# Layer 1's neighbourhood attention ends in spare places, the second gated tile is split later, and its buffers are dealt out anew

## The chip, the cores and the metric

The kernel runs on one core of a Trainium2 chip. The time is the device time of one execution in microseconds (us). TensorE is called PE, VectorE DVE, ScalarE ACT, GpSimd POOL, and SyncE, which issues most of the loads, SP. PEld is TensorE's loading of weights, which overlaps with its matmuls.

## The reference

Two layers of a transformer trunk with two token mixers side by side. The latent stream x has 512 tokens, the context 256, the model width is 1024. Each layer normalises and modulates, makes ten groups of columns with one projection, runs neighbourhood attention (NA) and grouped-query attention (GQA), multiplies each by a gate of its own, projects both, adds them under sigmoid gates and projects once more:

```python
    hx = _rmsnorm(x, norm_g) * (1.0 + scale_x) + shift_x
    px = hx @ w_in
    a_k, a_v, b_k, b_v, a_q, b_q, a_z, b_z, g_a, g_b = _split(px, SPLIT_SIZES)
    ...
    a_att = _na_latent(qa, ka, va, cka, cva, rpb, rows)     # 8 heads of 64, window 8 x 16, and all context keys
    b_att = _gqa_latent(qb, k_all, v_all)                   # 8 query heads, 2 key heads, 768 keys
    ...
    o_a = (a_att * jax.nn.silu(a_z)) @ w_o_a
    o_b = (b_att * jax.nn.silu(b_z)) @ w_o_b
    merged = jax.nn.sigmoid(g_a) * o_a + jax.nn.sigmoid(g_b) * o_b
    x_new = x + gate_x * (merged @ w_out)
```

Layer 0 also computes the context's tokens (update_ctx), with 256 rows more in every stage; layer 1 leaves them out after the keys and values. All is float32.

## The kernel before

**Split products.** PE multiplies operands of the rounded type fp32r. Each float32 operand is therefore split in a high part (an ACT cast to fp32r) and a low part (the rest, a subtraction on DVE or POOL), and each product is made of three matmuls, high by high, high by low and low by high (lines 352 to 354). Weights go through three places: a raw buffer that SP's load fills (`raw`, three buffers), `whi` and `wlo` (rings of eight each, in the pool `wp`). A raw buffer is free when the low part has read it. `load_w` (line 322 the cast, 325 the low part) loads tiles of 512 columns, `load_w2` (337 and 339) two tiles of 256 in one. `mix_lo` gives the low parts of weights to POOL and DVE by turns.

**Layers and stages.** Each layer goes through the projections for NA, NA itself, the projection BKV and BQ for GQA (lines 937 on; w_q is the weight of BQ), GQA, the projections w_o_a and w_o_b with the merge, and w_out. PE is kept busy during attention by pieces of other projections (`fill`): gate chunks, and in GQA the pieces of w_o_a. The flag `first` is true in layer 0.

**Attention.** `pipeline` runs the scores of head h, then the values of head h−1. Scores go to psum tiles `pss`, are reduced to a maximum, and exponentiated by ACT (line 815 for NA, 975 for GQA), four blocks of 128 queries to a head. `softmax_tail` normalises a block: DVE inverts the sum, then DVE (line 667) or POOL (669 and 670; the blocks 1 and 3 of each head) multiplies. `transpose_split` transposes four blocks on PE into a psum tile `pst` of two buffers, ACT casts it to `pth` (687) and DVE makes `ptl` (688); the value matmuls (837 to 848 for NA, 990 and 991 for GQA) add up in one psum tile `psv`. An NA head has four such tiles, two of 512 columns, then two of 448; a GQA head has six. `head_out` evacuates psv: an ACT copy of one half (696), a DVE add (698) and a product with the gate's values on POOL (699) into `za` or `zb`. The tile `ho` has one buffer, so the next copy waits for the product; psv has one buffer, so the next head's first value matmul waits for the add (in layer 0 the context's queries use it as well, lines 762 and 763).

In layer 1, the last head of GQA uses a *spare place* for every other one of its tiles (line 676): psum of the scores (`pss`), and `whi`/`wlo` from the weights' ring. So more than two transposed tiles can be under way. `att["end"]` switches it on.

**Gated tiles.** `hilo` splits the gated values za and zb in high (`gah`, `gbh`) and low (`gal`, `gbl`) parts, four pieces of 128 channels each, on ACT and POOL. These, `tg` (the gates), `gk`, `qb` and others have the same size (128 x 3072 float32) and share nine buffers (`big`): a new tile waits for the last reader of the one whose buffer it gets. `early` runs before the last head's values of GQA and splits the first three pieces of zb; the last piece follows after the pool of attention is closed.

**Order.** The instructions are emitted in program order and then placed by the framework's scheduler on each engine, which runs its own in sequence and waits for others by semaphores. `ordered(x, name)` ties an instruction behind another of the same engine, and makes it wait for nothing else. The numbers of buffers in a ring are dealt out in program order, so a tile that is allocated earlier in the program pushes all later tiles of its ring back.

## Time and profile before

| | us |
|---|---|
| median of 3 runs | 1142.38 (1141.61 to 1142.96) |
| profiled execution | 1141.48 |
| its span, first to last instruction | 1139.6 |
| PE busy | 1119.0 (98%) |
| DVE busy | 816.4 (72%) |
| ACT busy | 581.1 (51%) |
| POOL busy | 492.7 (43%) |
| moved by DMA | 135.09 MB, mean 119 GB/s |

Layer 0's attention ends near 560 us of the span, its merge lies behind that, layer 1's NA runs to about 883 us and its GQA to about 1070 us. A row of the timeline has the start, the duration, the engine, the source line, the operation, the tiles written and read, their size, and in brackets how long the engine was idle before it and what ended that. "x3" stands for three in a row. The durations of matmuls reach past the next one's start, as they are pipelined: the pace of PE is read from start to start.

### The profile page before, as it was taken

What the parts mean: (1) busy time and instruction counts of PE and PEld (TensorE: products, weight loads), DVE (VectorE), ACT (ScalarE), POOL (GpSimd) and SP (SyncE); (2) the same over time, 40 slices, a digit from 0 to 9 for tenths busy, and PEclk for the clock granted to TensorE, in tenths of its full rate; (3) what the DMA queues carried; (4) which work ended last, traced back from release to release, by engine and by line L of the source; (5) the groups of instructions that cost most, each with busy time, mean ns of one, the idle gap of its engine ahead of it and who ended that gap; (6) DMA issues with size and microseconds to landing.
All of it is one profiled execution on the core that took longest, in us unless ns stands there. A gap on an engine that the chain in (4) does not pass through costs nothing.

```text
span 1139.6 us, 17434 instructions
## 1 busy us (share of the span) xinstructions
PE 1119.0 (98%) x6128; PEld 947.5 (83%) x6128; DVE 816.4 (72%) x1537; ACT 581.1 (51%) x1185; POOL 492.7 (43%) x467
## 2 busy tenths in 40 slices
PE   7999999999999999999999999999999999999998
PEld 5788888888988888888888887888887988888777
DVE  6777688887554786698588755569787666798783
ACT  6553366665433565666330365337666445665531
POOL 2073354544374343353512427246553664363521
PEclk9999999999999999999999999999999999999999
DMA  9645222333333232461343524634332333141343
GB/s 370 238 127 157 81 61 70 97 115 98 114 102 89 91 108 87 80 242 38 137 141 102 176 75 116 188 91 125 103 111 74 112 94 110 66 157 38 99 163 99
DMA packets 90863, 135.09 MB, mean 119 GB/s; under 512 B 10804, under 2 KB 55064, under 8 KB 90136
## 3 DMA queue, kind: packets, MB, share of 16 engines
q1 hardware_dynamic: 88640, 127.57, 35.2%
q0 software_dynamic: 1856, 6.29, 1.7%
q8 instruction: 48, 0.79, 0.3%
q14 instruction: 39, 0.32, 0.1%
q10 hardware_dynamic: 280, 0.12, 0.0%
HBM read 116.63 MB, written 17.32 MB: 118 GB/s over the span
## 4 chain that ended last, share of the span: by engine, by line
PE 86%; DVE 5%; DMA 3%; issue 3%; POOL 2%; ACT 1%; SPq 0%; POOLq 0%; ACTq 0%; DVEq 0%
PE psx L352 12%; PE psx L354 12%; PE psx L353 12%; PE psf L352 10%; PE psf L354 10%; PE psf L353 10%; PE pst L683 5%; PE pss L807 3%; PE pss L734 2%; PE pss L735 2%; PE psv L990 2%; PE psv L991 2%; PE pst L432 1%; DMA rawb<-in_w_ada_dram 1%; DVE ptl L688 1%
## 5 line engine op out<-in xcount | busy, mean ns | idle before, releaser
L687 ACT CAST pth<-pst 128x512 fp32r<-128x512 f32 (+1 forms) x173 | 97.2, 576 | 96.4 <-PE pst L683 56.0
L688 DVE TENSOR_TENSOR ptl<-pst,pth 128x512 fp32r<-128x512 f32 (+1 forms) x173 | 113.8, 671 | 41.1 <-ACT pth L687 40.0
L339 POOL TENSOR_TENSOR wlo<-raw,whi 128x512 fp32r<-128x512 f32 x68 | 95.9, 1414 | 104.4 <-ACT whi L337 86.2
L352 PE MATMUL psf<-hx,whi 128*128 128x512 f32 (+1 forms) x368 | 140.1, 381 | 0.0
L353 PE MATMUL psf<-hx,whi 128*128 128x512 f32 (+1 forms) x368 | 138.0, 375 | 0.0
L352 PE MATMUL psx<-whi,hx 128*128 128x512 f32 (+1 forms) x368 | 137.8, 375 | 0.0
L354 PE MATMUL psf<-hx,wlo 128*128 128x512 f32 (+1 forms) x368 | 137.7, 374 | 0.0
L354 PE MATMUL psx<-whi,hx 128*128 128x512 f32 (+1 forms) x368 | 135.9, 369 | 0.0
L353 PE MATMUL psx<-wlo,hx 128*128 128x512 f32 (+1 forms) x368 | 135.3, 368 | 0.0
L337 ACT CAST whi<-raw 128x512 fp32r<-128x512 f32 x136 | 82.5, 621 | 55.9 <-DMA raw<-in_w_in_dram 36.5
L322 ACT CAST whi<-raw 128x512 fp32r<-128x512 f32 x88 | 54.0, 622 | 100.9 <-PE psx L354 35.3
L683 PE MATMUL pst<-ident,p 128*128 128x128 f32 x628 | 97.7, 272 | 0.8 <-DVE r L664 0.6
L669 POOL TENSOR_SCALAR r<-r 128x1 f32<-128x1 f32 x64 | 22.3, 348 | 164.1 <-DVE r L664 139.4
L339 DVE TENSOR_TENSOR wlo<-raw,whi 128x512 fp32r<-128x512 f32 x68 | 67.1, 989 | 32.9 <-ACT whi L337 32.6
L325 POOL TENSOR_TENSOR wlo<-raw,whi 128x512 fp32r<-128x512 f32 x36 | 50.7, 1413 | 85.6 <-ACT whi L322 72.4
L683 PEld LDWEIGHTS pst<-ident,p 128*128 128x128 f32 x628 | 76.4, 140 | 12.3 <-PE psv L763 0.7
L670 POOL TENSOR_TENSOR p<-p,r 128x512 f32<-128x512 f32 (+1 forms) x64 | 84.3, 1317 | 5.1
L352 PEld LDWEIGHTS psx<-whi,hx 128*128 128x128 f32 x368 | 69.4, 189 | 12.2 <-issue 1.2
L354 PEld LDWEIGHTS psx<-whi,hx 128*128 128x128 f32 x368 | 69.4, 189 | 12.0 <-DVE hx L1165 0.2
L354 PEld LDWEIGHTS psf<-hx,wlo 128*128 128x128 f32 x368 | 69.3, 188 | 11.8
L353 PEld LDWEIGHTS psx<-wlo,hx 128*128 128x128 f32 x368 | 69.5, 189 | 10.7
L352 PEld LDWEIGHTS psf<-hx,whi 128*128 128x128 f32 x368 | 69.4, 189 | 10.4 <-ACT zt L517 0.2
(265 smaller groups left out, 3068.6 us busy)
## 6 DMA issues: line engine op xcount, KB each, us to landing
raw<-in_w_in_dram SPq DMA_DIRECT2D x168, 256.0 KB, 2.9
rawb<-in_w_ada_dram SPq DMA_DIRECT2D x48, 256.0 KB, 2.9
gs<-zt SPq DMA_DIRECT2D x32, 256.0 KB, 2.0
raw<-in_w_out_dram SPq DMA_DIRECT2D x32, 256.0 KB, 3.0
tg<-gs SPq DMA_DIRECT2D x4, 1536.0 KB, 6.5
rawx<-in_w_ada_dram SPq DMA_DIRECT2D x8, 512.0 KB, 7.7
raw<-in_w_o_a_dram SPq DMA_DIRECT2D x16, 256.0 KB, 2.9
raw<-in_w_o_b_dram SPq DMA_DIRECT2D x16, 256.0 KB, 4.3
```

Source lines behind the costliest of these rows:

```text
L322: S.copy(hi[:, :n], raw[:, :n])
L325: e.tensor_tensor(lo[:, :n], raw[:, :n], F(hi[:, :n]), ALU.subtract)
L337: S.copy(hi, raw)
L339: lo_eng(i).tensor_tensor(lo, raw, F(hi), ALU.subtract)
L352: T.matmul(ps, lhs[0], rhs[0], start=first, stop=False)
L353: T.matmul(ps, lhs[0], rhs[1], start=False, stop=False)
L354: T.matmul(ps, lhs[1], rhs[0], start=False, stop=last)
L670: G.tensor_tensor(p[:, c0:c1], p[:, c0:c1], r[:, i:i + 1].to_broadcast([128, c1 - c0]), ALU.mult)
L683: T.transpose(pt[:, c0:c0 + 128], src, ident)
L687: S.copy(hi[:, n0:n1], pt[:, n0:n1])
L688: V.tensor_tensor(lo[:, n0:n1], pt[:, n0:n1], F(hi[:, n0:n1]), ALU.subtract)
L807: T.matmul(pss.rearrange("p (a b n) -> p a b n", a=2, b=2), qi, blocks_of(k, *at), start=b, stop=not b)
```

## The change

1. **Spare places at the end of layer 1's NA.** A new flag `att["last"]` is set when the last head of a pipeline has its values made, also in NA; the count of turns starts anew there. In layer 1 the tiles 1 and 3 of NA's head 7 so take psum of the scores and a `whi`/`wlo` pair. In layer 1, block 3 of head 7 is normalised by DVE, not by POOL.
2. **The split of zb.** In `early` the high parts are tied behind the last exponential of GQA (`att["exp"]`), the low parts behind POOL's last normalisation, in both layers (before: no tie for the high parts, and none for the low ones in layer 0). The last piece is split by column spans, in layer 0 512 and 256, with the low part on DVE in both layers, and the last head's products with zb are on DVE in both layers.
3. **Buffers.** `tg[3]` is allocated and loaded after the second chunk of w_o_b's weights has been asked for, not in `early`. `gbh`, `gbl` and what follows so get other buffers of the nine.
4. **w_o_b's casts.** Those of the chunks 1 to 3 are tied behind the last output copy in layer 0 too.

```diff
@@ -562,7 +562,7 @@
             for f in fs:
                 for a, b in parts or [(0, ntok)]:
                     S.copy(R(dst[0][:, f, a:b]), sv[:, f, a:b])
-                    if hi_after is not None and f > 0:
+                    if hi_after is not None:
                         ordered(ins[-1], hi_after)
                     lo(f).tensor_tensor(R(dst[1][:, f, a:b]), sv[:, f, a:b], dst[0][:, f, a:b], ALU.subtract)
                     if lo_after is not None and lo(f) is G:
@@ -673,7 +673,7 @@
 
             def transpose_split(blocks, n0=0, n1=512):
 
-                spare = att["end"] and not first and att["turn"] % 2 == 1
+                spare = (att["end"] or att["last"]) and not first and att["turn"] % 2 == 1
                 att["turn"] += 1
                 pt = psw(512, "s" if spare else "t")
                 for src, c0 in blocks:
@@ -696,7 +696,7 @@
                 S.copy(t1[m:m + 64, :n], po[o:o + 64, :n])
                 att["ho"] = nc.cur_bb.bb.instructions[-1].name
                 V.tensor_tensor(t1[m:m + 64, :n], po[m:m + 64, :n], t1[m:m + 64, :n], ALU.add)
-                (V if (att["end"] and not first) else G).tensor_tensor(dst, dst, t1[m:m + 64, :n], ALU.mult)
+                (V if att["end"] else G).tensor_tensor(dst, dst, t1[m:m + 64, :n], ALU.mult)
 
             def rows(a, half):
                 return a[64 * half:64 * half + 64]
@@ -814,7 +814,8 @@
                     r = sp.tile([128, 2], F32, tag="r", name=nm("r"), bufs=8)
                     S.activation(p[:, :512], p[:, :512], AF.Exp, bias=mx[:, 0:1], scale=-1.0,
                                  accum_out=r[:, 0:1])
-                    softmax_tail(p, 512, r[:, 0:1], [(0, 512)], G if i in NA_POOL else None)
+                    softmax_tail(p, 512, r[:, 0:1], [(0, 512)],
+                                 G if i in NA_POOL and (first or (h, i) != (7, 3)) else None)
                     ps_.append(p)
                     run(att["bg"], 1)
                 return ps_
@@ -856,6 +857,7 @@
                 prev = None
                 for h in range(8):
                     att["bg"] = bg if h > 3 or pm["n"] == 1 else []
+                    att["last"] = False
                     st = scores_of(h)
                     if prev is not None:
                         values_of(h - 1, prev)
@@ -865,12 +867,12 @@
                     run(fill, len(fill))
                     last()
                 run(bg, len(bg))
-                att["end"] = last is not None
+                att["end"], att["last"], att["turn"] = last is not None, True, 0
                 values_of(7, prev)
                 run(fill, len(fill))
 
             akt = [k_tile(e, True) for e in range(2)]
-            att["end"], att["turn"] = False, 0
+            att["end"], att["last"], att["turn"] = False, False, 0
 
             def na_first(h):
                 j, e = h // 2, h % 2
@@ -973,6 +975,7 @@
                     V.tensor_reduce(mx[:, 0:1], pss, AX, ALU.max, negate=True)
                     r = sp.tile([128, 2], F32, tag="r", name=nm("r"), bufs=8)
                     S.activation(p, pss, AF.Exp, bias=mx[:, 0:1], accum_out=r[:, 0:1])
+                    att["exp"] = next(x.name for x in nc.cur_bb.bb.instructions[::-1] if x.engine == ON_ACT)
                     softmax_tail(p, 768, r[:, 0:1], [(0, 768)], G if i in GQ_POOL else None)
                     ps_.append(p)
                     run(att["bg"], 1)
@@ -1001,11 +1004,10 @@
 
             def early():
 
-                for c in (1, 3):
-                    tg[c] = big("tg")
-                    load_tg(c)
+                tg[1] = big("tg")
+                load_tg(1)
                 gated["b"] = hilo_tiles("gb")
-                hilo(zb, gated["b"], range(3), lo_after=None if first else att["norm"])
+                hilo(zb, gated["b"], range(3), hi_after=att["exp"], lo_after=att["norm"])
             bg = gate_steps((1,), att["p"]) if first else []
             pipeline(fill, 8, gq_first, values_of(zb, gq_values), early, bg)
             gq_es.close()
@@ -1017,7 +1019,7 @@
             for v in range(nv):
                 src = gd[l][8 * v:8 * v + 8].rearrange("k p -> (k p)").unsqueeze(0)
                 nc.sync.dma_start(gv[:, v, :], src.to_broadcast([128, DM]))
-            hilo(zb, gated["b"], [3], None, lambda f: G if first else V)
+            hilo(zb, gated["b"], [3], spans, lambda f: V)
             mg = []
 
             def evac_b(f, n0, n1, ps):
@@ -1034,8 +1036,11 @@
                     at = len(nc.cur_bb.bb.instructions)
                     chunks[i + 1][0]()
                     for x in nc.cur_bb.bb.instructions[at:]:
-                        if not first and x.engine == ON_ACT:
+                        if x.engine == ON_ACT:
                             ordered(x, att["ho"])
+                if i == 0:
+                    tg[3] = big("tg")
+                    load_tg(3)
                 if i % 2 == 0:
                     mg.append(hilo_tiles("m"))
                 for piece in chunks[i][1]:
```

`ordered` is shown above, with `hilo`. The names of psum tiles say their place: `pst` is transposes' own, `pss` the scores'.

The first place is ACT in layer 1 at the end of NA: from head 7's last exponential (line 815) to head 7's output copy before the change. `pth` are the transposed tiles of heads 6 and 7, `ho` the output copies of heads 5, 6 and 7.

```order
L815 ACTIVATE p_2153_9465,r_2155_9468<-p_2153_9465,mx_2154_9466 128x512
L687 CAST pth_2158_9479<-pst_2157_9474 128x512
L696 COPY ho_2124_9366<-psv_2111_9317 64x512
L687 CAST pth_2161_9490<-pst_2160_9485 128x512
L687 CAST pth_2164_9501<-pst_2163_9496 128x448
L687 CAST pth_2167_9514<-pst_2166_9509 128x448
L687 CAST pth_2176_9588<-pst_2175_9583 128x512
L696 COPY ho_2169_9522<-psv_2156_9473 64x512
L687 CAST pth_2179_9599<-pst_2178_9594 128x512
L687 CAST pth_2182_9610<-pst_2181_9605 128x448
L687 CAST pth_2185_9623<-pst_2184_9618 128x448
L696 COPY ho_2187_9631<-psv_2174_9582 64x512
```

And there with the change, from the spare casts of head 7 to head 6's output copy:

```order
L687 CAST whi_2179_9600<-pss_2178_9595 128x512
L687 CAST whi_2185_9624<-pss_2184_9619 128x448
L337 CAST whi_2200_9715<-raw_2199_9713 128x512
L337 CAST whi_2203_9721<-raw_2202_9719 128x512
L337 CAST whi_2206_9727<-raw_2205_9725 128x512
L687 CAST pth_2164_9502<-pst_2163_9497 128x448
L687 CAST pth_2167_9515<-pst_2166_9510 128x448
L337 CAST whi_2209_9733<-raw_2208_9731 128x512
L322 CAST whi_2212_9739<-raw_2211_9737 128x512
L687 CAST pth_2176_9589<-pst_2175_9584 128x512
L322 CAST whi_2215_9745<-raw_2214_9743 128x512
L696 COPY ho_2169_9523<-psv_2156_9474 64x512
```

Head 7's tiles 1 and 3 are cast before head 6's two tiles of 448 columns; eight weight casts (L337 for BKV, L322 for w_q), which stood among the exponentials of heads 5 and 6 and just behind them, now follow the spare casts (six are in these rows).

The second place is ACT at the end of GQA in layer 1, around the last exponential (`p_2685`, L975 before and L977 after); `gbh` is the high part of zb. Before:

```order
L975 ACTIVATE p_2681_11616,r_2683_11619<-pss_2680_11611,mx_2682_11617 128x768
L564 CAST gbh_2713_11753<-zb_2338_10277 128x512 x2
L687 CAST pth_2651_11500<-pst_2650_11495 128x512
L687 CAST pth_2654_11511<-pst_2653_11506 128x512
L687 CAST pth_2657_11522<-pst_2656_11517 128x512
L975 ACTIVATE p_2685_11628,r_2687_11631<-pss_2684_11623,mx_2686_11629 128x768
L687 CAST pth_2660_11533<-pst_2659_11528 128x512
L687 CAST pth_2690_11642<-pst_2689_11637 128x512
L696 COPY ho_2662_11539<-psv_2643_11472 64x512
L687 CAST pth_2693_11653<-pst_2692_11648 128x512
L687 CAST whi_2720_11778<-pss_2719_11773 128x512
L687 CAST whi_2726_11800<-pss_2725_11795 128x512
```

With the change:

```order
L687 CAST pth_2651_11501<-pst_2650_11496 128x512
L687 CAST pth_2654_11512<-pst_2653_11507 128x512
L687 CAST pth_2657_11523<-pst_2656_11518 128x512
L977 ACTIVATE p_2685_11629,r_2687_11632<-pss_2684_11624,mx_2686_11630 128x768
L564 CAST gbh_2712_11752<-zb_2338_10278 128x512 x2
L687 CAST pth_2660_11534<-pst_2659_11529 128x512
L687 CAST pth_2690_11643<-pst_2689_11638 128x512
L687 CAST whi_2719_11777<-pss_2718_11772 128x512
L687 CAST whi_2725_11799<-pss_2724_11794 128x512
L696 COPY ho_2662_11540<-psv_2643_11473 64x512
L687 CAST pth_2693_11654<-pst_2692_11649 128x512
L687 CAST whi_2731_11821<-pss_2730_11816 128x512
```

The two casts of gbh have moved from ahead of three transposed tiles to right behind the last exponential, and two spare casts of head 7 (`whi` from `pss`) stand ahead of head 6's output copy.

The third place is POOL at the end of GQA in layer 0, from the last normalisations on; `gbl` is the low part of zb, L339 are low parts of w_o_b. Before:

```order
L669 TENSOR_SCALAR r_1383_6143<-r_1383_6143 128x1
L670 TENSOR_TENSOR p_1381_6140<-p_1381_6140,r_1383_6143 128x768
L699 TENSOR_TENSOR zb_931_4170<-zb_931_4170,ho_1356_6023 64x256
L339 TENSOR_TENSOR wlo_1469_6534<-raw_1467_6530,whi_1468_6532 128x512
L699 TENSOR_TENSOR zb_931_4170<-zb_931_4170,ho_1407_6229 64x512
L699 TENSOR_TENSOR zb_931_4170<-zb_931_4170,ho_1412_6247 64x256
L567 TENSOR_TENSOR gbl_1421_6326<-zb_931_4170,gbh_1420_6325 128x768 x3
L339 TENSOR_TENSOR wlo_1479_6614<-raw_1477_6610,whi_1478_6612 128x512
L699 TENSOR_TENSOR zb_931_4170<-zb_931_4170,ho_1441_6400 64x512
L699 TENSOR_TENSOR zb_931_4170<-zb_931_4170,ho_1446_6418 64x256
```

With the change:

```order
L669 TENSOR_SCALAR r_1383_6143<-r_1383_6143 128x1
L670 TENSOR_TENSOR p_1381_6140<-p_1381_6140,r_1383_6143 128x768
L567 TENSOR_TENSOR gbl_1420_6324<-zb_931_4170,gbh_1419_6323 128x768 x2
L699 TENSOR_TENSOR zb_931_4170<-zb_931_4170,ho_1356_6023 64x256
L567 TENSOR_TENSOR gbl_1420_6324<-zb_931_4170,gbh_1419_6323 128x768
L699 TENSOR_TENSOR zb_931_4170<-zb_931_4170,ho_1407_6229 64x512
L699 TENSOR_TENSOR zb_931_4170<-zb_931_4170,ho_1412_6247 64x256
L251 DMA rawb_1522_6849<-in_w_ada_dram 128x512
L339 TENSOR_TENSOR wlo_1456_6452<-raw_1454_6448,whi_1455_6450 128x512
```

The low parts of the first two pieces follow the last normalisation, those of w_o_b have moved behind the last products, and the products of the last head are gone from POOL.

## The prediction

> **What bounds the kernel now.** I read the page first for the engine that sets the time, then the stretches that the diff touches, by engine, then PE's waits by what ended them, and last the order of time inside three stretches. The page's first and fourth parts:
>
> ```profile
> PE 1119.0 (98%) x6128; PEld 947.5 (83%) x6128; DVE 816.4 (72%) x1537; ACT 581.1 (51%) x1185; POOL 492.7 (43%) x467
> ...
> PE 86%; DVE 5%; DMA 3%; issue 3%; POOL 2%; ACT 1%; SPq 0%; POOLq 0%; ACTq 0%; DVEq 0%
> ```
>
> TensorE is busy for 1119.0 of 1139.6 us, so all waits of the span together are 20.6 us. The change alters no matmul, only orders and engines; it can win no more than the part of these waits that lies where it acts, and it loses whatever new wait it makes. Where it acts: the end of GQA and the merge of layer 0, the end of NA in layer 1, the end of GQA in layer 1. The windows (start:end, length, then busy us of PE, PEld, DVE, ACT, POOL, clock, DMA share, GB/s):
>
> ```profile
> 545.00:560.00 15.00, 13.27 (x78) 10.76 (x75) 8.01 (x12) 5.79 (x11) 9.39 (x7) 1.00 0.11 38
> ...
> 840.00:890.00 50.00, 47.59 (x291) 40.66 (x291) 40.59 (x81) 31.26 (x67) 23.38 (x26) 1.00 0.27 84
> 1040.00:1070.00 30.00, 28.86 (x160) 22.75 (x159) 22.58 (x36) 19.62 (x38) 14.67 (x13) 1.00 0.11 36
> ```
>
> The clock is 1.00 throughout. PE's idle time is 15.00 − 13.27 = 1.73 us in the first (A), 2.41 in the second (B), 1.14 in the third (C): 5.3 us at stake. No other engine is full there, so what counts is the order in which ACT, DVE and POOL hand results to PE.
>
> **B: end of NA, layer 1.** The timeline of all engines (start, duration of one row, engine, line, tiles; in brackets the idle time before it and what ended it), cut to the rows I use, then the line of the page for the weight loads with its median to landing:
>
> ```profile
> 857.92 0.61 ACT L322 CAST whi<-raw 128x512 fp32r<-128x512 f32 x1
> 858.66 1.30 POOL L325 TENSOR_TENSOR wlo<-raw,whi 128x512 fp32r<-128x512 f32 x1 [5.45 <-PE psf L354]
> ...
> 864.51 0.40 PE L807 MATMUL pss<-kl,qs 128*128 128x512 f32 x1
> ...
> 865.84 0.47 PE L837 MATMUL psv<-pth,va 128*128 128x512 f32 x1 [0.93 <-DVE ho L698]
> ...
> 870.67 0.47 DVE L667 TENSOR_SCALAR p<-p,r 128x512 f32<-128x512 f32 x1
> ...
> 871.07 0.22 DVE L664 RECIPROCAL r<-r 128x1 f32<-128x1 f32 x2
> ...
> 871.22 0.69 DVE L811 CUSTOM_DVE_ANT_0 p<-pss,bint 128x512 f32<-128x512 f32 x1
> ...
> 871.96 0.72 ACT L815 ACTIVATE p<-p,mx 128x512 f32<-128x512 f32 x1 [0.87 <-DVE mx L811]
> ...
> 873.37 1.04 POOL L670 TENSOR_TENSOR p<-p,r 128x512 f32<-128x512 f32 x1
> ...
> 875.36 0.53 ACT L687 CAST pth<-pst 128x448 fp32r<-128x448 f32 x1 [0.83 <-PE psv L837]
> 875.40 0.39 PE L837 MATMUL psv<-pth,va 128*128 128x512 f32 x1
> ...
> 875.63 0.42 PE L838 MATMUL psv<-ptl,va 128*128 128x512 f32 x1
> ...
> 876.52 0.53 ACT L687 CAST pth<-pst 128x448 fp32r<-128x448 f32 x1 [0.62 <-PE pst L683]
> ...
> 878.33 0.58 ACT L696 COPY ho<-psv 64x512 f32<-64x512 f32 x1 [0.16 <-PE psv L848]
> ...
> 878.94 0.59 ACT L687 CAST pth<-pst 128x512 fp32r<-128x512 f32 x1
> 878.95 0.68 DVE L698 TENSOR_TENSOR ho<-psv,ho 64x512 f32<-64x512 f32 x1
> ...
> 882.91 0.31 PE L352 MATMUL psx<-whi,hx 128*128 128x256 f32 x1
> ```
> ```profile
> raw<-in_w_in_dram SPq DMA_DIRECT2D x168, 256.0 KB, 2.9
> ...
> raw<-in_w_o_b_dram SPq DMA_DIRECT2D x16, 256.0 KB, 4.3
> ```
>
> Here the tail of heads 6 and 7 runs at ACT's and DVE's pace: one transposed tile after the other, 876.52 − 875.36 = 1.16 us each, and the first BKV matmul that finds values done starts at 882.91. Two of head 7's four tiles now get spare places and are transposed before head 6 has ended; the last block is normalised by DVE in 0.47 us instead of 1.04 on POOL. That should take two turns of 1.16 us off. But the spare tiles are taken from the ring of eight of the weight tiles, and in the built order eight weight casts, done before this tail until now (one at 857.92 is quoted), stand behind them on ACT, in the midst of the tail. I follow them:
>
> - The last score maximum no longer stands behind a normalisation and reciprocals (870.67 to 871.22, 0.55 us), and I give it 0.3 more since its scores come without the BKV matmuls ahead of them: the exponential starts at about 871.96 − 0.85 = 871.1. With 0.72 of exponential, 0.15 of reciprocal (in the doubled row at 871.07, 0.22) and 0.47 it is normalised at about 872.45, not at 873.37 + 1.04 = 874.41. PE, in order, waits for it before the spare transposes. The wait at 865.84 (0.93; from 864.51 to it 1.33 instead of the usual 0.23, the step from 875.40 to 875.63) falls away, because other matmuls are put there; the 2.9 us of BKV matmuls that filled PE from 867 to 872 are now spread among the values of heads 6 and 7.
> - Transposes bring it to about 873.4. Spare casts, 0.59 and 0.53: 874.5. First weight cast, 0.61: 875.1. Its low part on POOL, 1.30: 876.4. Only now is the first of three raw buffers free, so that the fourth BKV load can start: 2.9 us to landing, 879.3.
> - ACT stands in order: that cast (0.61, 879.9), a w_q cast (880.5), head 7's first tile (0.59, 881.1), one more w_q cast (881.7), head 6's output copy (0.58, 882.3). DVE's add, 0.68: 883.0. Then head 7's twelve value matmuls: four of 512 columns, 0.23 from start to start, and eight of 192 or 256, which by their width I estimate at 0.11: 4 × 0.23 + 8 × 0.11 = 1.8, so 884.8.
>
> Against 882.91 that is +1.9; I take **B = +1.8**, since the tile of 448 that follows lies beside these matmuls. Without the wait for the load, the same queue of ACT from 874.5 (three weight casts, two tiles of 448, two weight casts, a tile, a cast, the copy: 5.9 us, then 0.68 and 1.8) gives 882.9, that is 0. Bounds: −2.4 (all the idle of the window gone) and +3.3, if the load takes 4.3 us as w_o_b's do (1.4 more). I take the upper middle, because 2.9 is the median of 168 such loads. The w_q weights behind them are late too; five more BKV tiles of 24 matmuls, at 0.12 each by their width 14 us, lie between 884.8 and their first use, and hide it. Without that cover each would cost a load, 2.9 us.
>
> **C: end of GQA, layer 1.**
>
> ```profile
> 1048.97 1.14 ACT L564 CAST gbh<-zb 128x512 fp32r<-128x512 f32 x2
> ...
> 1050.62 0.59 ACT L687 CAST pth<-pst 128x512 fp32r<-128x512 f32 x1 [0.51 <-PE psv L990]
> ...
> 1053.71 0.90 ACT L975 ACTIVATE p<-pss,mx 128x768 f32<-128x768 f32 x1
> ...
> 1054.60 1.31 ACT L687 CAST pth<-pst 128x512 fp32r<-128x512 f32 x2
> ...
> 1055.28 1.47 POOL L670 TENSOR_TENSOR p<-p,r 128x768 f32<-128x768 f32 x1
> ...
> 1056.55 0.58 ACT L696 COPY ho<-psv 64x512 f32<-64x512 f32 x1 [0.64 <-PE psv L991]
> ...
> 1057.16 0.69 DVE L698 TENSOR_TENSOR ho<-psv,ho 64x512 f32<-64x512 f32 x1 [0.52 <-ACT ho L696]
> ...
> 1057.90 0.50 PE L990 MATMUL psv<-pth,vb 128*128 128x512 f32 x1 [0.23 <-DVE ho L698]
> ```
>
> The two gbh casts (1.14 us) ran in time that ACT had free: it still waited 0.51 us after them. Now they are tied behind the last exponential, ahead of the two tile casts of 1054.60, and two spare casts (1.1 us) stand ahead of the output copy. So head 6's last tile is cast 1.14 us later, and the copy, released at 1056.55, goes behind the spare casts, whose transposes need the block that POOL normalises until 1056.75: those casts run from about 1057.4 to 1058.5, the copy to 1059.1, DVE's two low parts stand ahead of the add, which ends near 1060.0. PE's first matmul of head 7 thus starts at 1060.0 instead of 1057.90: 2.1 us. The transposes of one spare tile are moved ahead into that time (0.4) and the wait of 0.23 is in it: **C = +1.5**. Bounds 0 (if POOL's 1056.75 is what PE waits for either way) and +2.1. What would hide the casts, the idle ACT time before 1050.62, lies ahead of the exponential and can't be used any more. The low parts keep their place behind POOL's last normalisation, and tg's later load is needed only in the last two chunks: nothing.
>
> **A: end of GQA and merge, layer 0.**
>
> ```profile
> 550.85 5.88 POOL L567 TENSOR_TENSOR gbl<-zb,gbh 128x768 fp32r<-128x768 f32 x3 [3.60 <-PE psf L353]
> ...
> 556.78 0.50 PE L353 MATMUL psf<-gbl,whi 128*128 128x512 f32 x1 [0.79 <-POOL gbl L567]
> ...
> 558.05 1.28 POOL L699 TENSOR_TENSOR zb<-zb,ho 64x512 f32<-64x512 f32 x1
> ...
> 559.37 0.36 ACT L696 COPY ho<-psv 64x256 f32<-64x256 f32 x1 [3.08 <-POOL zb L699]
> ...
> 560.25 0.50 PE L352 MATMUL psx<-gbh,whi 128*128 128x512 f32 x1 [1.18 <-DVE ho L698]
> ```
>
> POOL starts the low parts at 550.85, since their buffer was that of gal, which o_a's last matmul frees. With tg's fourth buffer allocated later they get another one, and in the built order the first two follow POOL's last normalisation: the 0.79 at 556.78 goes. The nine o_b matmuls then run ahead of head 7's last values; the output copy and add come as much later, and PE waits there instead, to about 557.85 against 557.35 for the same point. Then DVE, not POOL, multiplies (about 0.69, as the add, for 1.28), so the 256 copy waits less: PE is at the row of 560.25 near 559.85. **A = −0.4.** Bounds: −1.7 (the window's idle gone) and +2, if the w_o_b casts, now behind the last output copy, and its loads, now among those of tg, gate and x, miss the third chunk.
>
> [...] The rows: an add of DVE on as many elements takes 0.69 (1057.16), but its product beside a low part on POOL took 1.81.
>
> ```profile
> 1072.02 1.29 POOL L339 TENSOR_TENSOR wlo<-raw,whi 128x512 fp32r<-128x512 f32 x1 [3.13 <-ACT whi L337]
> 1072.06 1.81 DVE L699 TENSOR_TENSOR zb<-zb,ho 64x512 f32<-64x512 f32 x1
> ```
>
> [...] By it A would be +0.7 and the sum 1.1 us higher. I don't take it: the first POOL low part needs a weight cast that stands on ACT behind the gbh cast, which needs the product.
>
> **Sum.** −0.4 + 1.8 + 1.5 = +2.9. The profiled execution took 1141.48 us, the median is 1142.38, 0.9 above it: 1144.4 on the first scale, **1145.3** on the second.
>
> **Rivals.**
>
> 1. *The spare places do what they are for* (faster). Place: the tail of B; it decides if ACT is through the third weight cast before head 6's 448 tiles are transposed, so that the casts fill its gaps (0.83 and 0.62 at 875.36 and 876.52). Then two turns of 1.16 us go, C is at its lower bound, A −0.4: −2.7, 1139.7. For it: ACT is idle for much of the tail. Against it: the fourth load can't start before a low part that itself follows the spares. 0.18.
> 2. *Waits only move.* The raw buffer is free early enough, B = 0, C near 1, A −0.4: +0.6, 1143.0. For it: PE is 98% busy, and each stall was there before in another form. 0.30.
> 3. *Loads become the bound*: B +3.3 by a load of 4.3 us, C 1.5, and A +2 by the third w_o_b chunk: +6.8, 1149.2. Against it: DMA share 0.27 and 0.11 in the windows. 0.12.
>
> My forecast has 0.40. About 0.2% (2.3 us) is what a measurement of this kernel can tell from no change. Faster: the first rival and a little, 0.20. Same: the second and the low edge of my forecast, 0.33. Slower: 0.47. The range leaves out the outer ends: 1139.5 to 1149.0; the forecast's own is 1143.5 to 1147.
>
> **What will show it.** In layer 1 the gbh casts stand right behind the last exponential and PE's first value matmul of head 7 near 1060 waits for ho (C right); the fourth BKV cast waits for its DMA, with head 7's tile behind it (B right), and the first psx matmul of BKV starts near 884.8 plus what earlier stages gave. POOL's first gbl near 533 and no PE wait on gbl shows A's step. Wrong: ACT's weight casts in the gaps, without a DMA wait, or head 7's values done before 882.9.

## The result and the profile after

The changed kernel takes 1150.61 us (median of 4 runs, 1148.73 to 1154.19), the kernel before 1142.34: a ratio of 1.0076, with a 95% interval of 1.005 to 1.0103. Run again on another occasion (e5) it took 1151.78 against 1142.02, ratio 1.0082 (1.0069 to 1.0095). It is slower by 8 to 10 us. That was the direction forecast, but three times the amount, and 1150.61 lies outside the range that ended at 1149.0.

The profiled execution is the fastest of the four, 1148.73 us, 7.25 above the profiled execution before. The page's first and fourth parts, and the windows (start:end, length, busy us of PE, PEld, DVE, ACT, POOL, clock, DMA share, GB/s) around the three places:

```profile
span 1146.6 us, 17419 instructions
...
PE 1121.3 (98%) x6128; PEld 949.7 (83%) x6128; DVE 819.4 (71%) x1542; ACT 580.2 (51%) x1186; POOL 485.5 (42%) x462
...
PE 85%; DVE 4%; DMA 3%; issue 3%; ACT 2%; POOL 1%; ACTq 0%; SPq 0%; POOLq 0%
```
```profile
545.00:560.00 15.00, 13.47 (x84) 11.60 (x83) 7.97 (x14) 5.36 (x10) 2.73 (x3) 1.00 0.39 130
560.00:575.00 15.00, 14.00 (x79) 12.23 (x80) 13.82 (x23) 5.85 (x12) 4.64 (x4) 1.00 0.87 297
840.00:892.00 52.00, 46.99 (x282) 39.85 (x281) 33.88 (x74) 30.26 (x63) 20.02 (x21) 1.00 0.22 70
```

In B, PE is idle for 5.0 us of 52, where it was 2.4 of 50. The starts of the same matmul in both timelines give the loss by place:

| the same PE instruction | before | after | later by |
|---|---|---|---|
| transposes near the start (L1126, now L1131) | 13.06 | 14.62 | 1.6 |
| value matmul near the end of layer 0's GQA (L990, now L993) | 534.11 | 535.38 | 1.3 |
| value matmul 6 us later (L990, now L993) | 540.57 | 542.87 | 2.3 |
| end of layer 0's wait region (L354, third o_b chunk's 256 columns) | 566.74 | 569.29 | 2.55 |
| matmul ahead of layer 1's last NA heads (L354) | 852.91 | 855.85 | 2.9 |
| first BKV matmul behind NA (L352) | 882.91 | 888.02 | 5.1 |
| GQA value matmul ahead of layer 1's last exponential (L990, now L993) | 1045.35 | 1050.92 | 5.6 |
| last GQA value matmuls of layer 1 (L991, now L994) | 1065.73 | 1072.48 | 6.75 |
| end of the span | 1139.6 | 1146.6 | 7.0 |

So 1.6 us came in the first 14 us, where the change has no line: four transposes there took 1.06 instead of 0.60. Other executions of the same lines do not have it (e5 and e2 start as before), so it is not the change's; 1.3 of it is left at 534. What is the change's in this execution is A +1.3, B +2.2 and C +1.2; 0.4 us come between A and B, 0.4 between B and C, and 0.2 behind C. Of A's 1.3, the first 1.0 comes between 534 and 541, ahead of the windows above. The other executions of the changed kernel are 1.0 to 5.5 us slower than this one; where those come from is told by the experiments.

Place A, all engines, from POOL's first low parts on:

```profile
533.93 3.70 POOL L567 TENSOR_TENSOR gbl<-zb,gbh 128x768 fp32r<-128x768 f32 x2
...
535.29 2.49 DVE L667 TENSOR_SCALAR p<-p,r 128x256 f32<-128x256 f32 x2
...
537.70 1.27 DVE L688 TENSOR_TENSOR ptl<-pst,pth 128x512 fp32r<-128x512 f32 x2
...
538.43 0.50 PE L994 MATMUL psv<-ptl,vb 128*128 128x512 f32 x1 [0.75 <-DVE ptl L688]
...
558.28 0.58 ACT L687 CAST pth<-pst 128x512 fp32r<-128x512 f32 x1 [2.63 <-PE pst L683]
558.89 0.58 ACT L696 COPY ho<-psv 64x512 f32<-64x512 f32 x1
...
559.62 0.69 DVE L698 TENSOR_TENSOR ho<-psv,ho 64x512 f32<-64x512 f32 x1
560.35 0.69 DVE L699 TENSOR_TENSOR zb<-zb,ho 64x512 f32<-64x512 f32 x1
...
560.37 0.39 PE L762 MATMUL psv<-pth,vb 128*128 128x256 f32 x1 [1.90 <-DVE ho L698]
...
562.20 0.49 PE L352 MATMUL psf<-gbh,whi 128*128 128x512 f32 x1 [0.63 <-ACT gbh L564]
```

The same two normalisations on DVE in the trace before, where POOL had nothing to do beside them:

```profile
534.08 0.61 DVE L667 TENSOR_SCALAR p<-p,r 128x256 f32<-128x256 f32 x2
```

The wait on gbl is gone, as forecast, and POOL starts gbl at 533.93. In its place stand three others. The first is 20 us earlier: beside POOL's early gbl, DVE takes 2.49 us for the two normalisations instead of 0.61, the low parts behind them start late, and PE waits 0.75 us for one. That is the 1.0 us between 534 and 541. The other two are at the merge, 1.90 us for ho and 0.63 for gbh. The product on DVE takes 0.69, not the 1.81 of the row at 1072.06 before, and nothing runs on POOL beside it: POOL stands idle for 12.48 us, until 562.76.

Place B, all engines and SP's queue:

```profile
873.97 0.49 DVE L667 TENSOR_SCALAR p<-p,r 128x512 f32<-128x512 f32 x1
...
875.33 1.30 POOL L699 TENSOR_TENSOR za<-za,ho 64x512 f32<-64x512 f32 x1 [1.16 <-DVE ho L698]
...
876.15 1.67 ACT L337 CAST whi<-raw 128x512 fp32r<-128x512 f32 x3
...
876.91 2.96 POOL L339 TENSOR_TENSOR wlo<-raw,whi 128x512 fp32r<-128x512 f32 x2 [0.28 <-POOL za L699]
...
877.33 1.40 DVE L339 TENSOR_TENSOR wlo<-raw,whi 128x512 fp32r<-128x512 f32 x1 [0.25 <-ACT whi L337]
...
878.76 0.39 SPq L334 DMA_DIRECT2D raw<-in_w_in_dram  x1
...
882.30 0.62 ACT L337 CAST whi<-raw 128x512 fp32r<-128x512 f32 x1 [3.61 <-DMA raw<-in_w_in_dram]
...
882.95 0.69 DVE L339 TENSOR_TENSOR wlo<-raw,whi 128x512 fp32r<-128x512 f32 x1 [3.15 <-ACT whi L337]
...
883.44 0.58 ACT L687 CAST pth<-pst 128x512 fp32r<-128x512 f32 x1
...
884.56 0.58 ACT L696 COPY ho<-psv 64x512 f32<-64x512 f32 x1
...
886.10 0.50 PE L838 MATMUL psv<-pth,va 128*128 128x512 f32 x1 [1.55 <-DVE ho L698]
...
888.02 0.30 PE L352 MATMUL psx<-whi,hx 128*128 128x256 f32 x1
```

And what SP's queue waited for, from 855 to 895:

```profile
SPq L334 <- DVE wlo L339: 10.1, 1, 10.1
```

This is the chain of the forecast, but for the engine of one row: a low part frees a raw buffer, the fourth load starts only at 878.76, ACT stands idle for 3.61 us on that DMA with head 7's tile and head 6's output copy behind it, and PE waits for ho. By the profile the low part that the load waited for is that of DVE at 877.33 (it ends 0.03 us before the load starts), not POOL's first. Beside POOL's low parts it takes 1.40 us; the next such one at 882.95, with POOL idle until 883.61, takes 0.69. So the load starts some 0.7 us later than it would with POOL idle, an estimate.

Place C in the trace after: the casts, the tiles, the spare casts, the copy, the add, PE.

```profile
1060.18 1.13 ACT L564 CAST gbh<-zb 128x512 fp32r<-128x512 f32 x2
...
1061.21 1.07 ACT L687 CAST pth<-pst 128x512 fp32r<-128x512 f32 x2
...
1062.74 1.07 ACT L687 CAST whi<-pss 128x512 fp32r<-128x512 f32 x2 [0.46 <-PE pss L683]
...
1063.84 0.58 ACT L696 COPY ho<-psv 64x512 f32<-64x512 f32 x1
...
1064.68 0.69 DVE L698 TENSOR_TENSOR ho<-psv,ho 64x512 f32<-64x512 f32 x1
...
1065.43 0.50 PE L993 MATMUL psv<-pth,vb 128*128 128x512 f32 x1 [0.67 <-DVE ho L698]
```

Here too the order is the one that was read from the built rows.

### The profile page after: what moved, and what is told of

Read it like the earlier page. It is cut to its first block, busy times and chain, and to the rows that moved or that the text cites. A ratio compares the mean times of both kernels' runs of the same rounds, so it can differ in the third digit from the quotient of the medians.

```text
span 1146.6 us, 17419 instructions
## 1 busy us (share of the span) xinstructions
PE 1121.3 (98%) x6128; PEld 949.7 (83%) x6128; DVE 819.4 (71%) x1542; ACT 580.2 (51%) x1186; POOL 485.5 (42%) x462
## 4 chain that ended last, share of the span: by engine, by line
PE 85%; DVE 4%; DMA 3%; issue 3%; ACT 2%; POOL 1%; ACTq 0%; SPq 0%; POOLq 0%
PE psx L352 11%; PE psx L354 11%; PE psx L353 11%; PE psf L352 10%; PE psf L354 10%; PE psf L353 10%; PE pst L683 5%; PE pss L807 2%; PE pss L734 2%; PE pss L735 2%; PE psv L994 2%; PE psv L993 2%; PE pst L432 1%; DMA rawb<-in_w_ada_dram 1%; DMA raw<-in_w_in_dram 1%
## 5 line engine op out<-in xcount | busy, mean ns | idle before, releaser
L339 POOL TENSOR_TENSOR wlo<-raw,whi 128x512 fp32r<-128x512 f32 x68 | 96.3, 1421 | 111.5 <-ACT whi L337 93.9
L352 PE MATMUL psf<-hx,whi 128*128 128x512 f32 (+1 forms) x368 | 140.1, 381 | 0.1
L352 PE MATMUL psx<-whi,hx 128*128 128x512 f32 (+1 forms) x368 | 137.9, 375 | 0.0
L354 PE MATMUL psf<-hx,wlo 128*128 128x512 f32 (+1 forms) x368 | 137.6, 374 | 0.0
L354 PE MATMUL psx<-whi,hx 128*128 128x512 f32 (+1 forms) x368 | 135.8, 369 | 0.0
L337 ACT CAST whi<-raw 128x512 fp32r<-128x512 f32 x136 | 82.2, 621 | 57.0 <-DMA raw<-in_w_in_dram 36.6
L322 ACT CAST whi<-raw 128x512 fp32r<-128x512 f32 x88 | 54.1, 623 | 101.1 <-DMA raw<-in_w_in_dram 34.3
L339 DVE TENSOR_TENSOR wlo<-raw,whi 128x512 fp32r<-128x512 f32 x68 | 67.1, 988 | 35.8 <-ACT whi L337 35.6
L670 POOL TENSOR_TENSOR p<-p,r 128x768 f32<-128x768 f32 (+1 forms) x63 | 82.9, 1316 | 5.0
L352 PEld LDWEIGHTS psx<-whi,hx 128*128 128x128 f32 x368 | 69.4, 189 | 12.1 <-issue 1.6
L354 PEld LDWEIGHTS psx<-whi,hx 128*128 128x128 f32 x368 | 69.4, 189 | 11.9
L354 PEld LDWEIGHTS psf<-hx,wlo 128*128 128x128 f32 x368 | 69.4, 188 | 11.8
L352 PEld LDWEIGHTS psf<-hx,whi 128*128 128x128 f32 x368 | 69.4, 189 | 10.5 <-ACT zt L517 0.3
```

Source lines behind the costliest of these rows:

```text
L322: S.copy(hi[:, :n], raw[:, :n])
L337: S.copy(hi, raw)
L339: lo_eng(i).tensor_tensor(lo, raw, F(hi), ALU.subtract)
L352: T.matmul(ps, lhs[0], rhs[0], start=first, stop=False)
L354: T.matmul(ps, lhs[1], rhs[0], start=False, stop=last)
L670: G.tensor_tensor(p[:, c0:c1], p[:, c0:c1], r[:, i:i + 1].to_broadcast([128, c1 - c0]), ALU.mult)
```

## The experiments

**Each place alone.** Three kernels take one place of the change each on the kernel before; a fourth takes B with another home for the spare tiles.

e1, layer 0 only (the new lines tg[3], ties, DVE, spans apply where `first`; the rows are cut):

```diff
...
-                for c in (1, 3):
+                for c in ((1,) if first else (1, 3)):
...
+                hilo(..., hi_after=att["exp"] if first else None, lo_after=att["norm"])
-                (V if (att["end"] and not first) else G).tensor_tensor(dst, ...)
+                (V if att["end"] else G).tensor_tensor(dst, ...)
-            hilo(zb, gated["b"], [3], None, lambda f: G if first else V)
+            hilo(zb, gated["b"], [3], spans if first else None, lambda f: V)
-                        if not first and x.engine == ON_ACT:
+                        if x.engine == ON_ACT:
+                if first and i == 0: tg[3] = big("tg"); load_tg(3)
```

> Only the edits of layer 0 (split of zb there, buffer of tg[3], casts of w_o_b, products on DVE) on the kernel before; layer 1 as before. Theory: the wait moves from gbl to psv and gbh, +0.5 to +1.0 us against before, narrow spread. Rival (the loads of w_o_b behind tg, gate and x are what makes the whole change slower and uneven): +3 to +5 us, runs several us apart.

e2, the lines with `att["last"]` and the block (7, 3) only:

> Only the end of layer 1's NA (spare places for tiles 1 and 3 of head 7, block 3 of head 7 on DVE). Theory: the fourth BKV load starts behind the first low part of the tail and holds up head 7, +2 to +3 us against before, with a wait of ACT on a DMA of over 2 us in the tail. Rival (the spare places do shorten the tail, the loss lies elsewhere): -2 to 0 us.

e3, only the tie of the high parts in layer 1:

```diff
...
-                hilo(zb, gated["b"], range(3), lo_after=None if first else att["norm"])
+                hilo(zb, gated["b"], range(3), hi_after=None if first else att["exp"],
+                     lo_after=None if first else att["norm"])
```

> Only layer 1's casts of gbh tied behind the last exponential of GQA. Theory: +1.3 to +1.6 us, PE's first value matmul of head 7 waits for ho some 2 us longer. Rival (POOL's last normalisation is what PE waits for either way): within 0.3 us of before.

e4, as e2, with

```diff
-                pool, th, tl, n = (wp, "whi", "wlo", 8) if spare else (att["p"], "pth", "ptl", att["nt"])
+                pool, th, tl, n = (((att["p"], "sph", "spl", 2) if att["last"] and not att["end"]
+                                    else (wp, "whi", "wlo", 8)) if spare else (att["p"], "pth", "ptl", att["nt"]))
```

> As the end of NA alone, but the spare high and low parts have two buffers of their own in the attention's pool instead of two of the weights' eight, so that the weight casts and loads need not wait for them. Theory: the ACT wait on the DMA goes and the values of head 7 end 3 us sooner than with the weights' ring: -1 to +0.5 us against before. Rival (the order of transposes and tiles is itself slower, whatever the loads do): as slow as the weights' ring, +2 to +3 us.

| run | median us (range) | ratio to before (95%) | against before (1142.21) |
|---|---|---|---|
| e1, A alone | 1144.73 (1143.76 to 1146.24) | 1.0021 (1.0012 to 1.003) | +2.5 |
| e2, B alone | 1147.29 (1146.9 to 1148.87) | 1.0045 (1.0032 to 1.0057) | +5.1 |
| e3, C alone | 1143.52 (1142.82 to 1144.77) | 1.0011 (1.0002 to 1.0019) | +1.3 |
| e4, B with buffers of its own | 1141.88 (1140.51 to 1143.06) | 0.9994 (0.9985 to 1.0003) | −0.3 |

2.5 + 5.1 + 1.3 = 8.9, against 8.3 and 9.8 of the whole: the places add up within the spread of the runs, and no large fourth one is left. (Layer 1's later tg[3] is in the whole and in none of the three.) C came out as forecast. e4 against e2 shows that B's loss is not in the spare places but in where they were taken from: with buffers of their own the weight casts stay ahead, no cast in the tail waits for a load, and 5.4 us are gone. But the gain that the spare places were to bring isn't there either: the wait has moved to psv, which head 7 needs and head 6's add frees.

```profile
878.43 0.59 ACT L687 CAST pth<-pst 128x512 fp32r<-128x512 f32 x1 [1.33 <-PE pst L683]
879.04 0.58 ACT L696 COPY ho<-psv 64x512 f32<-64x512 f32 x1
...
880.39 0.51 PE L838 MATMUL psv<-pth,va 128*128 128x512 f32 x1 [1.35 <-DVE ho L698]
```

(That is e4's timeline.) A and B were larger than the +1.3 and +2.2 of the first profile. The profiles of e1 and e2 show why; first e1's windows at the merge and e2's at the end of NA, then two matmul rows of e1 and the same matmuls of the whole change in its first profile:

```profile
555.00:560.00 5.00, 3.10 (x19) 2.44 (x18) 2.34 (x4) 1.16 (x2) 0.00 (x0) 1.00 0.65 250
560.00:565.00 5.00, 4.37 (x16) 3.59 (x16) 4.43 (x5) 2.85 (x6) 3.32 (x3) 0.54 0.77 283
565.00:570.00 5.00, 5.00 (x26) 4.34 (x25) 1.68 (x4) 0.00 (x0) 0.00 (x0) 0.78 0.93 307
```
```profile
880.00:884.00 4.00, 1.33 (x7) 0.93 (x7) 2.82 (x5) 3.35 (x6) 1.34 (x2) 1.00 0.31 82
884.00:888.00 4.00, 4.00 (x17) 3.63 (x18) 1.31 (x3) 1.48 (x3) 1.21 (x1) 0.57 0.43 133
888.00:892.00 4.00, 4.00 (x36) 4.00 (x35) 2.07 (x3) 2.19 (x5) 2.65 (x2) 1.00 0.67 204
```
```profile
562.75 0.63 PE L352 MATMUL psx<-gbh,whi 128*128 128x512 f32 x1
563.18 0.63 PE L353 MATMUL psx<-gbl,whi 128*128 128x512 f32 x1
```
```profile
563.13 0.39 PE L352 MATMUL psx<-gbh,whi 128*128 128x512 f32 x1
563.36 0.39 PE L353 MATMUL psx<-gbl,whi 128*128 128x512 f32 x1
```

Behind the waits the granted clock falls to 0.5 (e1's windows from 562 to 564 and from 564 to 566 both have 0.50). How long, can be estimated from the column of the clock, if it is either 1 or 0.5: 0.54 and 0.78 over 5 us each are 4.6 + 2.2 = 6.8 us of half clock in e1, 0.57 over 4 us is 3.4 us in e2. Meanwhile a matmul of 512 columns starts 0.43 us after the one before instead of 0.23. PE counts as busy all the while (4.00 of 4.00 in e2), so busy time hides this loss; the column of the clock and the number of matmuls show it. In e1, PE is 2.5 us late at the end of its waits and 4.2 us late at 566.74 (0.2 of both come from the start of the execution, and 1.0 from the wait behind DVE's normalisations, 0.74 us here). In e2, head 7's twelve value matmuls take from 883.91 to 887.31, 3.4 us, against 886.10 to 888.02, 1.9 us, in the first profile after, where the clock stayed at 1.00.

**The whole again, the wait filled, the old buffers, and psum for the last head.** e5 is the changed kernel as it is.

> The changed kernel as it is, once more. Theory (the three direct losses of about 1, 2.2 and 1.3 us, and on top, in some executions only, TensorE's granted clock falls to half for some us behind the waits of layer 0's merge or of layer 1's NA end): 1148 to 1154 us, in steps of about 2 us, and a profile that is slower than 1149 shows windows with a clock under 1.0 there. Rival (loads of uneven length make the spread): a slow profile shows clock 1.0 everywhere and longer waits on DMA.

1151.78 us (1150.08 to 1152.72). The profiled execution is again its fastest, 1150.08, and its windows have what the first profile lacks:

```profile
558.00:562.00 4.00, 2.49 (x10) 2.10 (x11) 3.16 (x6) 2.10 (x5) 0.14 (x1) 0.70 0.92 321
...
886.00:890.00 4.00, 3.53 (x15) 3.30 (x16) 1.86 (x4) 1.54 (x4) 1.28 (x1) 0.66 0.47 147
```

The clock fell at both places, and PE is 2.4 us late behind A and 6.4 us late at the first BKV matmul, without any loss at the start. So the same kernel pays for the clock in some executions and not in others, as the theory had it. The four runs of the first measurement agree, by the mean granted clock that is on record for each: 1.0 for 1148.73 us, 0.998 for 1149.69, 0.995 for 1151.53, 0.994 for 1154.19. The clock is not the only cause of a spread: e2's slowest run, 1148.87, has 1.0.

e6 is e1 with matmuls that nothing uses, in the place of the 1.9 us wait:

```diff
+                if att["end"]:
+                    spin = psw(1024, "s")
+                    for k in range(6):
+                        T.matmul(spin[:, :512], vsl(0), hi, start=True, stop=True)
                 po = psw(256, "v")
```

> Layer 0's edits alone, as in e1, with six matmuls of 128x512 into unused psum ahead of the context's last values, where PE waited 1.9 us for ho (their result is used by nothing). Theory (the wait itself brings the clock down): the clock stays at 1.0, the runs draw together at the low end of e1, 1143 to 1144 us, although PE does 1.4 us more. Rival (the clock falls whatever PE does there, or the loads set the spread): as e1 or slower, 1144.5 to 1146.5 us.

1144.71 us (1143.73 to 1146.9), ratio 1.0024 (1.0014 to 1.0034): as e1, and no narrower. In its profile the clock stays at 1.00 at the merge and PE is only 1.4 us late there, but it waits 1.7 us at the start of layer 1 for the normalised x, which was 0.2 in e1. The mean clock is 0.999 or 1.0 in eight of the nine runs, where six of e1's eleven have 0.997 or 0.998. So the filling seems to keep the clock up, but the median did not fall by it, and why not is open. In e1 itself the four runs with a clock of 1.0 have a median of 1143.83 (+1.6), the six with 0.997 or 0.998 one of 1145.16 (+2.9): the clock is worth some 1.3 us at A where it falls, an estimate.

e7 is e1 without the later buffer: tg[3] is allocated and loaded in `early`, as before.

```diff
-                for c in ((1,) if first else (1, 3)):
+                for c in (1, 3):
-                if first and i == 0: tg[3] = big("tg"); load_tg(3)
```

> Layer 0's edits alone without the later buffer of tg[3]: gbl keeps gal's buffer and starts behind o_a; PE's order then has the nine o_b matmuls behind head 7's value matmuls again. Theory (the early gbl lets the scheduler put nine matmuls, 2.1 us, ahead of the last values, so that the output copy and all behind it come later): within 0.7 us of before, no step. Rival (the casts of w_o_b behind the last copy, or the products on DVE, are the loss): +2 us and more, as e1.

1141.08 us (1140.46 to 1142.12), against 1142.02: ratio 0.9995 (0.9986 to 1.0004). All of A's loss is gone. PE's waits from 525 to 600, of e7 and then of the kernel before:

```profile
PE psf L353 <- POOL gbl L567: 0.7, 1, 0.7
PE psf L352 <- ACT gbh L564: 0.6, 1, 0.6
```
```profile
PE psx L352 <- DVE ho L698: 1.2, 1, 1.2
PE psf L353 <- POOL gbl L567: 0.8, 1, 0.8
```

gbl waits for o_a again and PE waits 0.7 us for it, the very wait that the new buffer was to remove. What the new buffer did instead is two things, both seen in the traces of e1, e5, e6 and the first profile and in neither e7 nor the kernel before. First, gbl runs beside DVE's normalisations, which take 2.49 us in the first profile and 0.61 in that of before; PE loses 1.0 us. In e1, e5 and e6 too POOL is busy for 3.26 to 3.29 of the 4.00 us from 534 to 538, and PE is idle for 0.74 or 0.75 of them; in e7 POOL is busy for 0.73 and PE is not idle there. Second, with gbl at hand all nine o_b matmuls were placed ahead of head 7's last value matmul. In e7 and before, four of the nine stand ahead of it and five behind:

```profile
555.50 0.47 PE L992 MATMUL psv<-ptl,vb 128*128 128x512 f32 x1
...
555.81 0.40 PE L353 MATMUL psf<-gbl,whi 128*128 128x512 f32 x1
```

(These are rows of e7's timeline.) Five matmuls at 0.23 are 1.15 us. From the start of the last four transposes ahead of the first o_b matmul it is 3.57 us to the last value matmul in e1 (553.32 to 556.89) and 2.46 in e7 (553.04 to 555.50). So everything that hangs on it, the tiles, the copy, the add, the product, gbh, came 1.1 us later, with nothing left to do meanwhile. With the old buffer these five stand behind the values and fill PE while the copy and the add run, and between 552 and 567 PE gains 0.9 us on the kernel before; with the new buffer it loses 0.2 there.

e8 is e4 with one line more, in the NA values:

```diff
-                po = psw(512, "v")
+                po = psw(512, "s" if att["last"] and not first else "v")
```

> As e4 (spare places with buffers of their own), and the last NA head of layer 1 adds up its values in the scores' third psum tile, so that its first value matmul need not wait for the add of head 6. Theory (in e4 the wait had only moved from the tiles to psv, 1.35 us): 1.0 to 1.5 us below e4, about 1140.7 us. Rival (the tail is set by ACT and DVE tile by tile): as e4.

1140.93 us (1140.25 to 1143.36), ratio 0.9991 (0.9982 to 1.0). Against its own runs of before that is −1.1, where e4 had −0.3: 0.8 better, less than the 1.0 to 1.5 expected, and the two intervals overlap. In the profile, waits of 0.9 and 0.3 for tiles remain.

**Both mended.** e9 has e7's layer 0 and e8's end of NA; the gbh casts of layer 1 stay where they were.

> Layer 0's edits with gbl's old buffer (as e7) and layer 1's NA end with spare buffers of its own and psum of the scores for the last head (as e8); layer 1's gbh casts where they were before. Theory (the places are apart, so the effects add: -0.9 and -1.1): about 1140 us, 2 us below before. Rival (what one place wins is lost in a later wait that is set by loads): 1141 to 1142 us.

1140.34 us (1139.87 to 1142.51) against 1142.26, ratio 0.9986 (0.9977 to 0.9995): 1.9 us faster than the kernel before, about the sum of 0.9 and 1.1. That is 0.14%, less than the 0.2% that the prediction took for what can be told, though the interval ends just below 1.

**A wait made longer.** e10 and e11 take the kernel before and repeat one copy, so that PE waits longer at the merge and nothing else is changed. e10 makes the copy four times, e11 eight times:

```diff
-                S.copy(t1[m:m + 64, :n], po[o:o + 64, :n])
+                for _ in range(4 if att["end"] and first and n == 512 else 1):
+                    S.copy(t1[m:m + 64, :n], po[o:o + 64, :n])
```

> The kernel before, with the 512-column output copy of layer 0's last GQA head made four times instead of once (the same values), so that PE waits some 1.7 us longer for psv at the start of the merge. Theory (a wait of about 2 us followed by another is what brings the granted clock down): in some runs 1.5 to 2 us more than the direct 1.7, that is 1143.5 to 1146 us, and if the profile is one of these, windows of clock 0.5 behind 558. Rival (the clock falls for a reason that lies in the changed kernel alone): 1143.5 us, clock 1.0.

> As e10 with eight copies, so that PE waits some 4 us longer. Theory: the clock falls in nearly every run and the profile shows half clock for 4 to 6 us behind the wait, 1146 to 1149 us. Rival: the direct 4 us alone, 1146 us, clock 1.0.

e10: 1143.93 us (1142.34 to 1145.49), spread over 3 us; its profile is the fastest run, 1142.34, with a wait of 1.4 us and the clock at 1.00. e11: 1146.25 us (1145.93 to 1146.81), with a wait of 3.9 us, and in its profile:

```profile
555.00:560.00 5.00, 2.14 (x11) 1.20 (x9) 0.69 (x1) 4.28 (x8) 3.37 (x3) 0.88 0.21 77
560.00:565.00 5.00, 3.20 (x14) 3.20 (x15) 1.12 (x2) 1.43 (x4) 2.18 (x3) 0.50 0.82 272
```

So a longer wait alone, in a kernel without the change, brings the clock down at the same place. The column of the clock puts the fall at 558.8 (0.88 over 5 us is 1.2 us of half clock, an estimate), 0.9 us after the wait began at 557.92. So 3.0 us of the slow time fall into the wait itself, and part of the rest into a wait that was there before (1.18 at 560.25), and e11 costs 4.0 and not more. All four runs of e11 have a mean clock of 0.996 to 0.998. For e10, that its slower runs are those with a lower clock is argued from e11 and e1, not shown, as only its fastest run was profiled. Its two fastest runs have a mean clock of 1.0 and the other eight 0.998 or 0.999, but the slowest of them has 0.999.

## Why the prediction was wrong

- **The direction and C were right.** C was put at +1.5: e3 measured +1.3. In e3's profile the last exponential starts 1.2 us late (1054.89 for 1053.71), in which the change has no part, and PE's first matmul of head 7 starts at 1061.03, that is 1059.85 on the clock of before; the forecast was 1060.0.
- **B was right in mechanism and mis-sized**: forecast +1.8, measured +5.1. The load was issued at 876.04 in e2, near the forecast 876.4, though the raw buffer was freed by DVE's low part, in 1.40 us beside POOL, and not by POOL's in 1.30. The step "2.9 us to landing, 879.3" failed first: the cast of that load starts at 880.12, 4.1 us after the issue; more loads are issued behind it from 876.48 on, which may be why, but no run shows it. That was the upper bound of the range (4.3), which I had set aside for the median of 168 loads. The value matmuls started at 883.91 instead of 883.0. The second failure is a term that the sum had not at all: these twelve matmuls took 3.4 us instead of 1.8, since the clock had fallen behind the waits. With +1.9 for the forecast chain, 0.9 and 1.6 make 4.4, PE's lateness at the first BKV matmul in e2. Near 894, where I had said that the other BKV tiles hide everything, 0.2 us more come in e2 and 0.4 in the first profile, and none in e5.
- **A had the wrong sign**: forecast −0.4, measured +2.5. Two steps failed. The first is a term put at nothing: that gbl may start early without a price. The forecast let "the first two follow POOL's last normalisation" and did not look at what DVE does beside them; its two normalisations take 2.49 us instead of 0.61 in the first profile, and PE loses 1.0. The longer product that it did weigh (1.81 beside a low part on POOL, where an add takes 0.69) was rightly set aside: at the merge it took 0.69, with POOL idle. The second is "PE waits there instead, to about 557.85 against 557.35". I had seen the nine matmuls move ahead, but carried them as a swap of one wait for another. Five of them moved and delay the whole chain behind the last values by 1.1 us, and this chain, not gbl, is the longest at that place. Against e7, where DVE's product stays and gbl is late, the merge loses 1.1 us; against the kernel before, 0.2. Together that is +1.2 to +1.3 at the full clock (first profile and e6). The rest of +2.5 goes with the clock in e1's slower runs; that it is all of the rest is not shown, since e6 has the clock up and the same median. The rival that blamed w_o_b's loads for an A of +2 was not what happened: no PE wait there ends on them.
- **The rivals.** That the spare places shorten the tail (0.18) needed casts in the gaps of ACT; the fourth load forbade it, as said against it. e4 shows that even without this the gain is 0.3 us or nothing. "Waits only move" had B at 0, and B was the largest loss. "Loads become the bound" gave 1149.2, nearest to the result; its load of 4.3 us came close to e2's 4.1, but its B of +3.3 was still short, and its A of +2 had the wrong reason.
- **The range** ended at 1149.0, 1.6 below the result. At the full clock, the first profile's losses without the start's 1.3 are 5.7 us, which on 1142.34 would be some 1148.0, an estimate: twice the forecast's +2.9, but inside the range. What carried the result beyond it is the clock: every term was worked out at the full clock. "The clock is 1.00 throughout" was true of the kernel before, whose waits behind the start were up to 1.2 us; I treated it as a property of the place and not of the waits.

## What to carry to other kernels

When a tile is moved into a ring that another stage uses, follow what the ring's later tiles feed: here two spare tiles in the weights' ring pushed eight casts, and through three raw buffers one load, into the most exposed place of the layer, and the row that freed the buffer was on DVE beside POOL, at twice its length (1.40 us for 0.69). When something is made ready earlier, look at what the scheduler then puts ahead: matmuls that fill a gap are worth most behind the chain that makes the gap, and moving them ahead of it turns the gap into a wait (here 0.9 us gained against 0.2 lost). Look also at what DVE does while POOL runs the work that was made ready earlier (here 2.49 us for 0.61). And let a new wait on PE of 2 us cost more than its length in the upper bound, since the clock may fall behind it: in e1 PE was 2.5 us late at the end of its waits and 4.2 us late at 566.74.

## What was not expected of the hardware

TensorE's granted clock falls to half behind waits that are short. In e1 the longest single wait was 1.90 us, with 0.63 soon after; in e2 waits of 1.23, 0.34 and 1.55 us ended between 880.78 and 883.91, and PE was busy for 1.33 of the 4.00 us from 880 to 884. Afterwards the clock was at 0.5 for some 6.8 us in e1 and 3.4 us in e2, estimates from its column. The same 1.90 and 0.63 at the merge left it at 1.00 in the first profile of the changed kernel, as did waits of 0.7, 0.3 and 1.5 us at the end of NA, and in the profile of the kernel before, waits of up to 1.2 us behind the start did not bring it down. So one kernel pays in one execution and not in the next. What decides it is not shown: no wait of e1 or e2 was as long as the slow time behind it, and PE was partly busy in between; and e11's wait is 3.9 us long, but the clock fell 0.9 us into it.

DVE beside POOL was slower than the forecast allowed, in its normalisations and in its low parts. Two normalisations of 256 columns (one tile and one column of factors) took 2.49 us beside POOL's gbl in the first profile and 0.61 without it in the profile of before. A low part took 1.40 us beside POOL's and 0.69 without (877.33 and 882.95 in the first profile).
